# Half of the second weight sums of a seven-product matrix product taken from accumulating DMA to VectorE, with the sums of x and the down passes moved

## The chip, the cores and the metric

The kernel runs on one core of a Trainium2 chip. The time is the device time of one execution in microseconds, and the median of several runs is compared. TensorE (PE in the profile) multiplies; VectorE (DVE), ScalarE (ACT) and GpSimd (POOL) work beside it, and SyncE (SP) issues most of the DMAs. Each engine executes its own instructions in order.

## The reference, cut to what matters

One layer of a trunk on 256 tokens of width 2048, in float32. Two SwiGLU feed-forward stages of width 5632 stand at its ends, with a mixer (a recurrent and an attention branch) between them. The change touches only the feed-forward stages:

```python
def _swiglu(x, w1, w3, w2):
    return (jax.nn.silu(x @ w1) * (x @ w3)) @ w2

x = _layer_norm(ALPHA * x + 0.5 * _swiglu(x, ffn1_w1[i], ffn1_w3[i], ffn1_w2[i]), ln1_g[i], ln1_b[i])
mix = _hybrid_mixer(x, w_in[i], b_gates_m[i], conv_m[i], norm_m[i], w_up_m[i], w_up_sb[i], w_out[i])
x = _layer_norm(ALPHA * x + mix, ln2_g[i], ln2_b[i])
x = _layer_norm(ALPHA * x + 0.5 * _swiglu(x, ffn2_w1[i], ffn2_w3[i], ffn2_w2[i]), ln3_g[i], ln3_b[i])
x = x + jax.nn.sigmoid(x @ w_ple_gate[i]) * (p[i] @ w_ple_proj[i])
```

## The kernel before

Every float32 factor is split into a high and a low part (`hi`, `lo`) of a type that TensorE multiplies faster, and a product of two factors is three matmuls: hi by hi, hi by lo and lo by hi (L1057 to L1059). A weight comes from HBM by DMA as a tile `raw` of 128 x 1024 values, ACT copies it to the high part (L1006) and VectorE subtracts to get the low one (L1010). A **unit** is one weight tile against one half of the tokens: six matmuls, 128 x 512 each.

The width 5632 is cut into eleven chunks of 512. Chunks 0 and 5 are computed plainly: gate (`w1`), then hidden (`w3`). The other nine go through `seven` (L312), which takes the two token halves and the two matrices `w1` and `w3` together as a 2 by 2 block product and forms it with seven products in place of eight. For each of the four **quads** `i` of 512 rows:

- product 1 takes the tile `t`, a quarter of `w1`, as loaded;
- product 5 takes T1: after the split for product 1, `w1.then` adds a quarter of `w3` to `t` in place by an accumulating DMA from GpSimd's queue (`grow`, L328);
- product 6 takes T2: after the split for product 5, `w5.then` adds a second quarter of `w3` to `t`, in the same way;
- product 2 takes a second quarter of `w1` (`b21`), product 4 the sum of `t` and `b21`, made by VectorE (`plus`, L333);
- products 7 and 3 take two quarters of `w3`, one after a sum by VectorE (L333 too).

Products 5, 6, 7 and 3 multiply sums of x in place of x. `form_turn` (L277) forms these sums once per stage and chunk of x, 18 + 5c units of planned time after chunk c of x is transposed (`DELAY["form"]`, L275), by four small VectorE operations, and splits them (L258, L259).

After the last unit of product 5, ACT copies bank E to `e` (L454) and VectorE writes X minus E into the bank B (L448), which product 6 then accumulates onto. Three empty places (`None`, L358) stand between products 5 and 6.

The list `main` (L504) holds the rest of the stage: the plain chunks and the down passes. A down pass `down(c)` multiplies the hidden values of chunk c (transposed by `turn`, L425, to tiles of `hT`) by `w2`, for four column groups `g`, and adds the outcome to `xres` on VectorE (L494): eight additions a pass. `down(5, 7)` sums two chunks in one pass. Before, there are nine passes: 0; 1; 2; 3; 4; 6; 5 and 7; 8 and 9; 10. `weave` (L155) puts the list of the seven-product chunks (`chained`, L352) between the units of `main` in even spacing, empty places counted.

The order of all instructions is written out by the program itself: it walks the list, keeps a planned time (`sched.now`, 1.30 for each unit), and issues turns, transposes and sums when they are due; where a unit needs a tile that isn't made yet, `sched.until` issues what is queued first. Splits are issued up to seven weights ahead (`SPLIT_FFN`). `loads` (L972) issues the weight DMAs ahead as long as pages are left: the pages of activation tiles, the raw tiles and two for each split must stay below `PAGES`, 44. A raw tile counts until the split that frees it (`frees`). A weight whose tile must first be summed has `make`, called while the weight before it or the one before that is split (`make(j + 1)`, `make(j + 2)`); `after` holds it back until another weight is split.

Of the kernel before, what the change touches and what calls it, by code (L numbers as in the profile page):

```python
# [24 lines left out]

PAGES = 44
TEMP_BUFS = 6


RAW_FFN, RAW_MIX, RAW_EDGE = 12, 5, 4  # L30
# [9 lines left out]


DELAY = {
    "after": 14.0, "form": 18.0, "ln_turn": 5.0, "ln_step": 1.7, "h": 8.0, "silu": 6.0, "late": 9.0, "rest": 1.2, "mt": 3.2,
    "sbt": 4.6, "g0": 3.0, "g1": 4.0, "g2": 12.0, "cv0": 1.0, "cv1": 3.5, "cv2": 1.3,
    "m0": 3.0, "m1": 0.6, "m2": 0.6, "m3": 4.6, "m4": 4.6, "s0": 6.6, "s1": 6.7, "s2": 5.0,
}
# [123 lines left out]
def flat(pairs):  # L170
    return [u for p in pairs for u in p]
# [7 lines left out]
def kernel(  # L179
# [7 lines left out]
    x, out = x[0], out[0]  # L187
# [5 lines left out]
    page_pool = ctx.enter_context(tc.tile_pool(name="page", bufs=PAGES))  # L193
    temp_pool = ctx.enter_context(tc.tile_pool(name="temp", bufs=TEMP_BUFS))
    small = ctx.enter_context(tc.tile_pool(name="small", bufs=4))
# [6 lines left out]
    sched = Sched()  # L202
    temps = [0]

    def temp():
        sched.until(lambda: temps[0] < TEMP_BUFS)
        temps[0] += 1
        return temp_pool.tile([P, COL], F32, name="temp", tag="temp")
# [10 lines left out]
    pages = [0]  # L219
# [41 lines left out]
    def transposed(src, act, c, t):  # L261
        ps = misc([P, 4, P])
        for k in range(4):
            nc.tensor.transpose(ps[:, k], src[:, k * P:(k + 1) * P], ident[:])  # L264
        dst = act.get(c, t)
        nc.scalar.copy(dst[:, 0], ps[:])  # L266
        if act.forms:
            if c not in act.whole:
                act.whole[c] = big()
                pages[0] += 1  # L270
            nc.scalar.copy(act.whole[c][:, t * COL:(t + 1) * COL], ps.rearrange("q k s -> q (k s)"))
        nc.vector.tensor_tensor(out=dst[:, 1], in0=ps[:], in1=dst[:, 0], op=ALU.subtract)  # L272
        act.mark(c, t, 4)
        if act.forms and all(act.ready(c, h) for h in range(TT)):
            sched.spawn(form_turn(act, c), DELAY["form"] + 5.0 * c)  # L275

    def form_turn(act, c):  # L277

        a = [act.whole[c][:, t * COL:(t + 1) * COL] for t in range(TT)]
        s12, s34 = temp(), temp()  # L280
        l, r = slice(0, 2 * P), slice(2 * P, 4 * P)
        nc.vector.tensor_tensor(out=s12[:, l], in0=a[1][:, l], in1=a[1][:, r], op=ALU.subtract)
        nc.vector.tensor_tensor(out=s12[:, r], in0=s12[:, l], in1=a[0][:, l], op=ALU.subtract)
        nc.vector.tensor_tensor(out=s34[:, l], in0=a[0][:, l], in1=a[1][:, l], op=ALU.subtract)
        nc.vector.scalar_tensor_tensor(out=s34[:, r], in0=a[0][:, r], scalar=-1.0, in1=s12[:, r],
                                       op0=ALU.mult, op1=ALU.subtract)
        yield 4.0
        pages[0] -= 1
        for h, src in enumerate((s12, s34)):
            dst = act.forms.get(c, h)  # L290
            split_psum(dst[:, 0], dst[:, 1], src.rearrange("q (k s) -> q k s", s=P))
            drop()
            act.forms.mark(c, h, 4)
# [18 lines left out]
    def seven(wa, wb, rows, col0, cols, act, done):  # L312

        n = rows // (4 * P)
        banks = {k: {} for k in "XEBW"}

        def unit(m, i, tile, src, half, sub, bank, first):
            u = Unit(tile, half, banks[bank], src, i, sub, first and i == 0, i == n - 1,
                     lambda ps, t, m=m: done(m, banks))
            u.onto = not first  # L320
            return u

        def quarter(w, i, sub):
            return rows_of(w, (4 * i + sub) * P, col0, cols)

        def grow(raw, src):
            def load():
                nc.gpsimd.dma_start(out=raw.tile[:, :, :cols], in_=src.src, accum_op=ALU.add)  # L328
            return load

        def plus(a, b):
            def make():
                nc.vector.tensor_tensor(out=a.tile[:, :, :cols], in0=a.tile[:, :, :cols], in1=b.tile[:, :, :cols],  # L333
                                        op=ALU.add)
            return make

        one, five, six, two, four, rest = [], [], [], [], [], []
        for i in range(n):
            t, b21 = quarter(wa, i, 0), quarter(wa, i, 2)
            w1, w5, w6 = Weight(t, [t], []), Weight(t, [], []), Weight(t, [], [])  # L340
            w1.then, w5.then = grow(t, quarter(wb, i, 0)), grow(t, quarter(wb, i, 2))
            one.append(unit(1, i, w1, act, 0, 0, "X", True))
            five.append(unit(5, i, w5, act.forms, 0, 0, "E", True))
            six.append(unit(6, i, w6, act.forms, 0, 2, "B", False))
            two.append(unit(2, i, Weight(b21, [b21], []), act, 0, 2, "X", False))
            four.append(unit(4, i, Weight(t, [], [t, b21], plus(t, b21)), act, 1, 2, "E", False))
            b12, b22 = quarter(wb, i, 0), quarter(wb, i, 2)
            rest.append(unit(7, i, Weight(b12, [b12, b22], [b12], plus(b12, b22)), act.forms, 1, 0, "W", False))
            rest.append(unit(3, i, Weight(b22, [], [b22]), act.forms, 1, 2, "B", False))
        return one, five, six, two, four, rest  # L350

    def chained(parts):  # L352

        out = list(parts[0][0])
        for j, (_, five, six, two, four, rest) in enumerate(parts):
            ahead = list(parts[j + 1][0]) if j + 1 < len(parts) else []
            n = len(five)
            out += five + [None] * 3 + six + two[:1]  # L358
            for i in range(n):
                out += two[i + 1:i + 2] + four[i:i + 1] + (ahead[i - 2:i - 1] if i >= 2 else [])  # L360
            ahead = ahead[n - 2:]
            for i, u in enumerate(rest):
                out += [u] + ahead[i:i + 1]
        return out
# [56 lines left out]
    def ffn(w1, w3, w2, act, norm, skew=True, ahead=()):  # L421
# [67 lines left out]
        def down(*chunks):  # L489
            pairs = []  # L490
            for g in range(D // COL):
                def add(ps, t, g=g):
                    xs = xres[t][:, g * COL:(g + 1) * COL]
                    nc.vector.scalar_tensor_tensor(out=xs, in0=ps, scalar=0.5, in1=xs,  # L494
                                                   op0=ALU.mult, op1=ALU.add)
                    if n - 1 in chunks:
                        norm.chunk(t, g)
                pairs += group(w2, [c * COL + r for c in chunks for r in (0, 2 * P)], g * COL, COL, hT, add)
            return pairs

        gate, hidden = zip(*(up(c) for c in (0, 5)))
        program.extend((skewed(gate[0][:SKEW]) if skew else flat(gate[0][:SKEW])) + flat(gate[0][SKEW:]))
        rest, tail = down(8, 9), down(10)
        main = flat(hidden[0] + gate[1] + down(0) + down(1) + down(2) + down(3) + down(4) + hidden[1] + down(6) + down(5, 7))  # L504
        program.extend(main[:8] + weave(main[8:] + flat(rest[:8]), chained([up7(c) for c in (1, 2, 3, 4, 6, 7, 8, 9, 10)])))
        program.append(norm.load)
        program.extend(ahead)
# [307 lines left out]
    for n in (4, 4, 4, 4, 4, 2):  # L815
        program.extend(flat(group(w_in, range(0, D, 2 * P), sq0 + first * DS, n * DS, x1T,
                                  lambda ps, t, f=first, n=n: sb_columns(ps, t, f, n))))
# [138 lines left out]
    pos = {"load": 0, "split": 0, "at": 0, "raw": 0}  # L956

    def mixing():
        j = pos["split"]
        return any(-EDGE <= j - e < EDGE for e, _ in edges) or [m for e, m in edges if e <= j][-1:] == [True]  # L960

    def limits(j):

        if any(-EDGE <= j - e < EDGE for e, _ in edges):
            return RAW_EDGE, SPLIT_EDGE
        mixer = [m for e, m in edges if e <= j][-1:] == [True]
        return (RAW_MIX, SPLIT_MIX) if mixer else (RAW_FFN, SPLIT_FFN)
# [3 lines left out]

    def loads(most=len(raws)):  # L972
        while (pos["load"] < most and pos["raw"] < (4 if pos["at"] < 6 else limits(pos["split"])[0])
               and (mixing() or pages[0] + pos["raw"] + 2 * limits(pos["split"])[1] < PAGES)):
            j = pos["load"]
            r = raws[j]
            r.tile = page_pool.tile([P, 2, COL], F32, name="raw", tag="page")
            for ks in pieces(j):
                nc.sync.dma_start(out=r.tile[:, ks, :r.cols], in_=r.src[:, ks])
                if j == 0 and ks.start == 0:  # L980
                    load_x(0, 1)
            if r.plus is not None:
                nc.gpsimd.dma_start(out=r.tile[:, :, :r.cols], in_=r.plus, accum_op=ALU.add)
            pos["load"] += 1
            pos["raw"] += 1
# [111 lines left out]
```

## Time and profile before

| | |
|---|---|
| median of 3 runs | 2329.43 us (2327.81 to 2337.3) |
| profiled execution, its own time | 2336.99 us |
| span of its instructions | 2335.2 us |
| mean granted TensorE clock | 0.979 |
| first feed-forward stage, seven-product part | about 45 to 720 us |
| second one | about 1510 to 2175 us |

PE busy counts a matmul from its issue to its end, and matmuls overlap, so the share of busy time is not that of the peak. A row of a wait says which instruction waited, for which, for how long in all, how many times and how long at most. The granted clock is 1.00 at full speed.

### The profile page before, as it was taken

How to read it: one execution, taken by the hardware profiler on the slowest of the kernel's cores; microseconds unless marked ns; L12 is line 12 of the kernel's file. 1: busy time of each engine (PE TensorE's matmuls, PEld its weight loads, DVE VectorE, ACT ScalarE, POOL GpSimd, SP SyncE). 2: the span in 40 equal slices, each digit the busy share in tenths (PEclk: the TensorE clock that was granted, in tenths of full speed). 3: DMA queues.
4: the chain of work that ended last, by engine and by line, in shares of the span. 5: the costliest groups of instructions: out<-in, count | busy, mean ns of one | idle time of the engine just before them, and what ended most of it. 6: DMA issues, size and time to landing. Idle time of an engine off the chain costs nothing.

```text
span 2335.2 us, 27582 instructions
## 1 busy us (share of the span) xinstructions
PE 2229.2 (95%) x10017; PEld 1833.4 (79%) x10017; DVE 1730.4 (74%) x1884; ACT 1259.3 (54%) x1471; POOL 223.3 (10%) x191
## 2 busy tenths in 40 slices
PE   9899999999899999999999999999899999988999
PEld 7677877887777788888888888777787787777878
DVE  6888898897787765654445456888788889778883
ACT  6655565664564455544643453556556566555552
POOL 3111111111000000100100000311110111100000
PEclk9999999999999999999999999999999999999999
DMA  9778988989795565565566577578897798978643
GB/s 325 213 219 244 283 241 224 263 222 278 220 284 183 172 190 160 174 185 157 163 189 191 178 237 234 158 208 234 238 284 224 228 263 232 269 219 263 240 148 104
DMA packets 267208, 510.21 MB, mean 218 GB/s; under 512 B 16000, under 2 KB 25024, under 8 KB 267072
## 3 DMA queue, kind: packets, MB, share of 16 engines
q1 hardware_dynamic: 227904, 432.95, 56.3%
q0 software_dynamic: 39168, 75.51, 18.0%
q8 instruction: 78, 1.28, 0.2%
q14 instruction: 58, 0.48, 0.1%
HBM read 506.30 MB, written 2.10 MB: 218 GB/s over the span
## 4 chain that ended last, share of the span: by engine, by line
PE 52%; issue 15%; DMA 6%; DVE 3%; POOL 2%; ACT 0%; POOLq 0%; ACTq 0%; DVEq 0%
PE mm L1057 15%; PE mm L1059 15%; PE mm L1058 15%; DMA raw<-in_ffn_w_dram 5%; POOL raw L328 2%; PE seeded L1057 2%; PE seeded L1058 2%; PE seeded L1059 1%; PE ms L264 1%; DVE split L1010 1%; DVE xres L403 1%; DMA temp<-in_conv_m_dram 0%; DVE xres L401 0%; DVE xres L404 0%; ACT split L1006 0%
## 5 line engine op out<-in xcount | busy, mean ns | idle before, releaser
L1010 DVE TENSOR_TENSOR split<-raw,split 128x1024 fp32r<-128x1024 f32 (+1 forms) x1037 | 1212.6, 1204 | 350.7 <-ACT split L1006 329.0
L1006 ACT CAST split<-raw 128x1024 fp32r<-128x1024 f32 (+1 forms) x1037 | 1038.1, 1037 | 619.1 <-DMA raw<-in_ffn_w_dram 164.9
L1057 PE MATMUL mm<-split,actT 128*128 128x512 f32 (+2 forms) x2704 | 1059.0, 392 | 18.5 <-ACT actT L258 12.8
L1059 PE MATMUL mm<-split,actT 128*128 128x512 f32 (+2 forms) x2704 | 1049.0, 388 | 12.3 <-DVE actT L272 11.5
L1058 PE MATMUL mm<-split,actT 128*128 128x512 f32 (+2 forms) x2704 | 1047.5, 387 | 5.5 <-DVE split L1010 5.4
L1057 PEld LDWEIGHTS mm<-split,actT 128*128 128x128 f32 x2704 | 513.1, 190 | 121.2 <-ACT actT L258 14.5
L1059 PEld LDWEIGHTS mm<-split,actT 128*128 128x128 f32 x2704 | 512.4, 190 | 121.8 <-DVE actT L272 16.9
L1058 PEld LDWEIGHTS mm<-split,actT 128*128 128x128 f32 x2704 | 513.2, 190 | 106.8 <-DVE split L1010 8.3
L328 POOL DMA_DIRECT2D raw<-in_ffn_w_dram x144 | 175.2, 1228 | 1079.3 <-DVE split L1010 822.3
L1057 PE MATMUL seeded<-split,actT 128*128 128x512 f32 x432 | 177.7, 411 | 52.8 <-DVE seeded L448 52.8
L333 DVE TENSOR_TENSOR raw<-raw 128x1024 f32<-128x1024 f32 x144 | 175.4, 1218 | 54.8 <-DMA raw<-in_ffn_w_dram 54.8
L1058 PE MATMUL seeded<-split,actT 128*128 128x512 f32 x432 | 175.3, 406 | 4.7 <-DVE split L1010 4.7
L1059 PE MATMUL seeded<-split,actT 128*128 128x512 f32 x432 | 173.9, 403 | 0.0
L1057 PEld LDWEIGHTS seeded<-split,actT 128*128 128x128 f32 x432 | 85.0, 197 | 75.2 <-DVE seeded L448 57.8
L266 ACT CAST actT<-ms 128x512 fp32r<-128x512 f32 x84 | 49.1, 588 | 105.7 <-PE ms L264 89.3
L1058 PEld LDWEIGHTS seeded<-split,actT 128*128 128x128 f32 x432 | 85.1, 197 | 24.2 <-DVE split L1010 7.3
L494 DVE SCALAR_TENSOR_TENSOR xres<-mm,xres 128x512 f32<-128x512 f32 x144 | 97.9, 683 | 6.5 <-PE mm L1059 6.5
L1059 PEld LDWEIGHTS seeded<-split,actT 128*128 128x128 f32 x432 | 84.8, 196 | 18.3
L272 DVE TENSOR_TENSOR actT<-ms,actT 128x512 fp32r<-128x512 f32 x84 | 57.1, 684 | 25.2 <-ACT actT L266 13.7
L418 POOL TENSOR_SCALAR xres<-xres 128x512 f32<-128x512 f32 x16 | 28.7, 1836 | 320.0 <-DVE xres L401 300.5
L236 ACT ACTIVATE temp<-mm 128x512 f32<-128x512 f32 (+1 forms) x36 | 20.7, 576 | 48.9 <-PE mm L1059 48.9
L236 ACT ACTIVATE big<-mm 128x512 f32<-128x512 f32 x20 | 12.0, 598 | 55.8 <-PE mm L1059 55.8
(124 smaller groups left out, 641.3 us busy)
## 6 DMA issues: line engine op xcount, KB each, us to landing
raw<-in_ffn_w_dram SPq DMA_DIRECT2D x527, 512.0 KB, 7.9
raw<-in_w_in_dram SPq DMA_DIRECT2D x168, 512.0 KB, 3.8
raw<-in_ffn_w_dram POOLq DMA_DIRECT2D x144, 512.0 KB, 9.7
raw<-in_w_out_dram SPq DMA_DIRECT2D x32, 512.0 KB, 5.2
raw<-in_w_ple_gate_dram SPq DMA_DIRECT2D x24, 512.0 KB, 4.7
raw<-in_w_up_m_dram SPq DMA_DIRECT2D x16, 512.0 KB, 3.7
raw<-in_w_up_sb_dram SPq DMA_DIRECT2D x16, 512.0 KB, 4.3
raw<-in_w_ple_gate_dram SPq DMA_DIRECT2D x16, 256.0 KB, 4.5
```

The lines of the kernel that those rows point to most:

```text
L236: nc.scalar.activation(out, in_, func, **kw)
L266: nc.scalar.copy(dst[:, 0], ps[:])
L272: nc.vector.tensor_tensor(out=dst[:, 1], in0=ps[:], in1=dst[:, 0], op=ALU.subtract)
L328: nc.gpsimd.dma_start(out=raw.tile[:, :, :cols], in_=src.src, accum_op=ALU.add)
L333: nc.vector.tensor_tensor(out=a.tile[:, :, :cols], in0=a.tile[:, :, :cols], in1=b.tile[:, :, :cols], op=ALU.add)
L418: nc.gpsimd.tensor_scalar(out=xs, in0=xs, scalar1=ALPHA, scalar2=None, op0=ALU.mult)
L494: nc.vector.scalar_tensor_tensor(out=xs, in0=ps, scalar=0.5, in1=xs, op0=ALU.mult, op1=ALU.add)
L1006: nc.scalar.copy(hi[:, ks], r[:, ks])
L1010: nc.vector.tensor_tensor(out=lo[:, ks], in0=r[:, ks], in1=hi[:, ks], op=ALU.subtract)
L1057: nc.tensor.matmul(ps, hi, w[0][:, k, :u.cols], start=first, stop=False, skip_group_check=u.onto)
L1058: nc.tensor.matmul(ps, hi, w[1][:, k, :u.cols], start=False, stop=False, skip_group_check=u.onto)
L1059: nc.tensor.matmul(ps, lo, w[0][:, k, :u.cols], start=False, stop=last, skip_group_check=u.onto)
```

## The change

- T2 of the quads 1 and 3 of each chunk is no longer formed by an accumulating DMA. The quarter of `w3` is loaded to a tile of its own by a plain DMA from SP's queue, and VectorE adds it to `t` (`plus`, L333) after the split for product 5. Quads 0 and 2 stay as they were.
- The sums of x are due 14 + 3c after the transposes in place of 18 + 5c.
- Eight empty places (`FORMED`) stand between product 1 and product 5 of the first seven-product chunk.
- The down passes become eight: 0 and 1; 2; 3; 4; 6 and 5; 7; 8 and 9; 10. (The nine before are named above.)
- Weight loads stop one page sooner (`SPARE`).

```diff
+FORMED = 8
+SPARE = 1
...
-    "after": 14.0, "form": 18.0, "ln_turn": 5.0, "ln_step": 1.7, "h": 8.0, "silu": 6.0, "late": 9.0, "rest": 1.2, "mt": 3.2,
+    "after": 14.0, "form": 14.0, "ln_turn": 5.0, "ln_step": 1.7, "h": 8.0, "silu": 6.0, "late": 9.0, "rest": 1.2, "mt": 3.2,
...
-            sched.spawn(form_turn(act, c), DELAY["form"] + 5.0 * c)
+            sched.spawn(form_turn(act, c), DELAY["form"] + 3.0 * c)
...
             w1, w5, w6 = Weight(t, [t], []), Weight(t, [], []), Weight(t, [], [])
-            w1.then, w5.then = grow(t, quarter(wb, i, 0)), grow(t, quarter(wb, i, 2))
+            w1.then = grow(t, quarter(wb, i, 0))
+            if i % 2:
+                b = quarter(wb, i, 2)
+                w6 = Weight(t, [b], [b], plus(t, b), w5)
+            else:
+                w5.then = grow(t, quarter(wb, i, 2))
...
-        out = list(parts[0][0])
+        out = list(parts[0][0]) + [None] * FORMED
...
-        main = flat(hidden[0] + gate[1] + down(0) + down(1) + down(2) + down(3) + down(4) + hidden[1] + down(6) + down(5, 7))
+        main = flat(hidden[0] + gate[1] + down(0, 1) + down(2) + down(3) + down(4) + hidden[1] + down(6, 5) + down(7))
...
-               and (mixing() or pages[0] + pos["raw"] + 2 * limits(pos["split"])[1] < PAGES)):
+               and (mixing() or pages[0] + pos["raw"] + 2 * limits(pos["split"])[1] < PAGES - SPARE)):
```

## The prediction

> **What bounds the kernel now.** I read the busy times first, then who TensorE waits for, then the places of those waits in order of time.
>
> ```profile
> span 2335.2 us, 27582 instructions
> ...
> PE 2229.2 (95%) x10017; PEld 1833.4 (79%) x10017; DVE 1730.4 (74%) x1884; ACT 1259.3 (54%) x1471; POOL 223.3 (10%) x191
> ```
>
> TensorE (PE) is the bound. A gain can only come from its gaps or from the time in which its clock is low. The waits of PE over the whole span:
>
> ```profile
> PE seeded L1057 <- DVE seeded L448: 52.8, 12, 6.6
> PE mm L1057 <- ACT actT L258: 12.8, 3, 7.9
> PE mm L1059 <- DVE actT L272: 11.5, 10, 2.7
> PE mm L1057 <- ACT actT L266: 5.7, 4, 2.5
> PE mm L1058 <- DVE split L1010: 5.4, 5, 2.0
> PE seeded L1058 <- DVE split L1010: 4.7, 5, 1.7
> ```
>
> The columns are microseconds in all, times, longest. The largest is the wait for L448, which seeds the bank of product 6 (X minus E) after product 5. It strikes 12 of the 18 seven-product chunks. What is late there is seen in chunk 4, in the timelines of PE, DVE, ACT and POOL:
>
> ```profile
> 296.89 0.80 PE L1057 MATMUL seeded<-split,actT 128*128 128x512 f32 x1 [5.52 <-DVE seeded L448]
> ...
> 296.14 0.69 DVE L448 TENSOR_TENSOR seeded<-mm,temp 128x512 f32<-128x512 f32 x1
> ...
> 284.94 1.05 ACT L1006 CAST split<-raw 128x1024 fp32r<-128x1024 f32 x1 [5.29 <-DMA raw<-in_ffn_w_dram]
> ...
> 288.96 1.05 ACT L1006 CAST split<-raw 128x1024 fp32r<-128x1024 f32 x1 [2.44 <-DMA raw<-in_ffn_w_dram]
> 292.79 1.99 ACT L1006 CAST split<-raw 128x1024 fp32r<-128x1024 f32 x2 [2.78 <-DMA raw<-in_ffn_w_dram]
> 294.69 0.58 ACT L454 COPY temp<-mm 128x512 f32<-128x512 f32 x1
> ...
> 276.80 1.20 POOL L328 DMA_DIRECT2D raw<-in_ffn_w_dram  x1 [17.20 <-DVE split L1010]
> 279.07 2.44 POOL L328 DMA_DIRECT2D raw<-in_ffn_w_dram  x2 [1.07 <-DVE split L1010]
> ```
>
> The four accumulating DMAs that form T2 are issued within some 6 us. They land one after another, 4.0 and 3.8 us apart (284.94, 288.96, 292.79). ACT works in order: the copy of E (L454, 0.58 us) stands behind the split of the third T2 and starts at 294.69. PE had run dry at 296.89 - 5.52 = 291.37. So the third landing of four sets the end of this wait.
>
> A stall costs twice, since the granted clock (next to last but two columns) is halved after it. Here are the first and the last of the nine slow stretches behind L448 waits, and the sum of the nine:
>
> ```profile
> 147.91:150.63 2.72, 2.72 (x6) 2.14 (x7) 2.72 (x4) 1.12 (x2) 0.00 (x0) 0.50 0.03 6
> ...
> 2128.89:2134.20 5.31, 5.31 (x13) 4.15 (x14) 4.35 (x5) 2.99 (x3) 0.00 (x0) 0.50 0.07 27
> sum 37.80, PE 37.79 PEld 29.63 DVE 34.80 ACT 19.96 POOL 0.00; mean PE 4.20 PEld 3.29 DVE 3.87 ACT 2.22 POOL 0.00
> ```
>
> 37.8 us at 0.50 lose half: 18.9 us. The first of them also gives the pitch: 2.72 us for 6 matmuls is 0.453 each at half clock, 0.227 at full clock, and 1.36 us for a unit of six.
>
> **T2 of the odd quads.** 36 accumulating DMAs go, two of four in each chunk; 36 plain loads on SP's queue and 36 sums at L333 come. The sums' price and what the fewer down passes return (16 fewer L494):
>
> ```profile
> L333 DVE TENSOR_TENSOR raw<-raw 128x1024 f32<-128x1024 f32 x144 | 175.4, 1218 | 54.8 <-DMA raw<-in_ffn_w_dram 54.8
> ...
> L494 DVE SCALAR_TENSOR_TENSOR xres<-mm,xres 128x512 f32<-128x512 f32 x144 | 97.9, 683 | 6.5 <-PE mm L1059 6.5
> ```
>
> 36 x 1.218 - 16 x 0.683 = 32.9 us more VectorE work. The third T2 (quad 2) becomes the second of two accumulations, so it lands about one interval sooner, 3.8 us. Twelve waits of 52.8 / 12 = 4.4 us mean would leave 0.6 us each; but the short ones can't give 3.8:
>
> ```profile
> 510.16 0.50 PE L1057 MATMUL seeded<-split,actT 128*128 128x512 f32 x1 [1.55 <-DVE seeded L448]
> ...
> 147.91 0.79 PE L1057 MATMUL seeded<-split,actT 128*128 128x512 f32 x1 [2.68 <-DVE seeded L448]
> ```
>
> So the long ones keep more. I leave 13 us in all: **-40**, between -15 (worked out under the first rival) and -53. Of the slow clock I take 15 of 18.9: **-15** (ends 4 and 19). The 2.68 us wait was followed by the slow stretch at 147.91; the 1.55 us wait was not (its first matmul took 0.50, not 0.79).
>
> The Trainium skill (TensorE: Matmul & The Clock Gate, Part 1) has the clock halve after an idle window of about 3.4 us. The 2.68 us row was slow already, so the trace bears the rule out only roughly. By it, leftover waits of about 1 us cost no clock at all, and this term would be -19.
>
> The new sums lie on VectorE before product 6, where it idles for ACT (60.6 us in this stretch, and 26.9 for DMA):
>
> ```profile
> 45.00:720.00 675.00, 630.85 (x2729) 514.26 (x2727) 566.68 (x559) 396.87 (x427) 86.51 (x71) 0.96 0.87 248
> ...
> L1010 DVE TENSOR_TENSOR split<-raw,split 128x1024 fp32r<-128x1024 f32 x349 | 415.3, 1219 | 74.2 <-ACT split L1006 60.6 <-PE mm L1059 7.6 <-PE mm L1058 2.7
> L333 DVE TENSOR_TENSOR raw<-raw 128x1024 f32<-128x1024 f32 x72 | 87.7, 1218 | 26.9 <-DMA raw<-in_ffn_w_dram 26.9
> ```
>
> VectorE is busy 566.7 of 675 us; 16 more in a stage some 22 us shorter is 583 of 653, 89%. I charge **+3** (0 to +33, if it were the bound all along). A sum stands in VectorE's FIFO ahead of splits and of L448, all of which wait if its b is late.
>
> **SP's queue and pages.** Each added load takes a page until its split, and SPARE takes one page off what may be loaded ahead. PE's waits for L1010 (5.4 + 4.7 = 10.1 us, in ten) show what late weights cost now. I charge half of it again, **+5** (0 to +20: twice what is there). For it speak 36 shorter transfers:
>
> ```profile
> q1 hardware_dynamic: 66675, 129.38, 55.9%
> q0 software_dynamic: 19505, 37.59, 30.9%
> ```
>
> Of 675 us of the 16 DMA engines that is 1.53 us for each plain 0.524 MB and 2.91 for each accumulating one.
>
> **Sums of x sooner, product 5 later.** Chunk 1's product 5 waits for the sums of x:
>
> ```profile
> 66.79 0.80 PE L1057 MATMUL mm<-split,actT 128*128 128x512 f32 x1 [7.87 <-ACT actT L258]
> ...
> 66.12 1.13 ACT L258 CAST actT<-temp 128x512 fp32r<-128x512 f32 x2
> ...
> 66.79:72.56 5.77, 5.65 (x12) 3.69 (x13) 5.67 (x10) 3.13 (x5) 0.00 (x0) 0.50 0.44 81
> ...
> 1529.28:1533.30 4.02, 3.41 (x8) 2.44 (x9) 3.76 (x5) 2.46 (x3) 0.00 (x0) 0.63 1.00 214
> ```
>
> The delay falls from 18 + 5c to 14 + 3c: 4, 6, 8 and 10 us sooner. Counted along the program list, eight empty places move the first unit of product 5 from place 31 to 36: five units of 1.36 us, 6.8 us. For sum 2, which is 7.87 us late, that makes 14.8. At stake: 12.8 plus slow clock of 2.9 and 4.02 x 0.37 = 1.5, in all 17.2. ACT's splits of T2 stand ahead of L258 too, so not all goes: **-15** (-8 to -17).
>
> **Down passes.** Joined passes need their second chunk sooner. Counting units between a chunk's last product and its first down unit: chunk 4 goes from 9 to 4, chunk 3 from 19 to 11, chunk 9 from 13 to 12, and chunk 1 from 41 to 3 (less the unit itself: two matmul units, 2.7 us). Chunk 4 shows what too few units cost:
>
> ```profile
> 366.02 0.55 PE L1057 MATMUL mm<-split,actT 128*128 128x512 f32 x1 [1.82 <-ACT actT L266]
> 368.11 0.80 PE L1059 MATMUL mm<-split,actT 128*128 128x512 f32 x1 [1.11 <-DVE actT L272]
> 369.98 1.05 PE L264 MATMUL ms<-ident,temp 128*128 128x128 f32 x4
> 371.71 0.80 PE L1057 MATMUL mm<-split,actT 128*128 128x512 f32 x1 [0.67 <-ACT actT L266]
> 371.08 0.58 ACT L266 CAST actT<-ms 128x512 fp32r<-128x512 f32 x1 [1.16 <-PE ms L264]
> ...
> 371.71:376.20 4.49, 4.49 (x11) 3.31 (x12) 2.81 (x4) 1.04 (x1) 0.00 (x0) 0.50 0.28 73
> ```
>
> 3.6 us of waits and 2.2 of slow clock, 5.8. Its L266 stood behind a T2 split, which now comes sooner; against that it has 5 units less: **0** (-8 to +8). Chunk 1 gets the same wait new. First half: transposes 0.6, L266 0.58 and L272 0.68 leave 1.8 exposed. Second half: L481 (0.68) comes first, with one split (1.2) ahead of it, 3.1. With 1.5 of slow clock that is 6.4 in each of the two feed-forward stages: **+13** (0, if the order hides it, to +22). Chunks 3 and 9 are forced slightly early in their second half, about 1 us each: **+4** (0 to +8). down(6, 5) leaves 12 units, 16 us, for chunk 5's transposes, due at 8 and 10: 0.
>
> **Sum:** -40 - 15 + 3 + 5 - 15 + 0 + 13 + 4 = **-45 us**. The profiled execution took 2336.99 us (1.8 outside its span), so 2292; it lies 7.6 above the median of the runs shown, 2329.43, from which the same difference gives **2284**.
>
> **Rivals.** *The DMA engines are shared anyway.* The b loads run in the very window of the accumulations, where the engines are full:
>
> ```profile
> 208.00:222.00 14.00, 9.37 (x44) 7.43 (x42) 8.52 (x10) 5.69 (x8) 1.20 (x1) 0.91 0.97 230
> 222.00:252.00 30.00, 29.42 (x124) 24.21 (x125) 29.25 (x31) 18.42 (x19) 2.41 (x2) 0.93 0.58 169
> ```
>
> Then T2 lands sooner only by 2.91 - 1.53 = 1.4 us: 12 x 1.4 gives -17 for -40 and -4 for the clock, in all -11: **2318**. Against it: pages limit the loads, so a b takes the place of another load there. This is what the Trainium skill says of queues (DMA: Bandwidth & Descriptors, Issuing engines are not separate DMA queues): all issuers share 16 engines. The 0.97 at 208 us agrees; whether a b displaces another load no row shows. Chance 0.14.
>
> *VectorE becomes the bound.* It has 29.25 of 30 us in the stretch from 222. If the added 33 us came fully on the path: -45 + 30 = -15, **2314**. Against it: 8.52 of 14 us just before, where the sums stand. Chance 0.11.
>
> *The b loads are as late as the DMA they replace, without more*: L448 gains nothing, -15 + 25 = +10, **2339**. Chance 0.10.
>
> *Slower: the new sum waits at the head of VectorE's queue for its b.* L333's waits cost 54.8 us in 20, 2.74 each; one page less makes b late. 26 of 36 late give 71 - 45 = +26, **2355**; it decides against the change from 17 late ones on (17 x 2.74 = 47). For it: those 20 waits exist, seldom on PE's path. Chance 0.09.
>
> **How the numbers follow.** The forecast has 0.56, with a range of 2260 to 2308. The 80% range is **2250 to 2322**: at the low end L448, clock and sums of x give all they have (-53 - 19 - 17 + 17 + 3 - 8 = -77, 2252); the first two rivals lie inside, the last two are left out. Half a per cent, about what a measurement here tells from no change, is 11.6 us. The first rival lies on that bound and is halved: faster 0.56 + 0.07 + 0.07 = 0.70; within 0.07 + 0.04 + 0.08 = 0.19; slower 0.02 + 0.09 = 0.11.
>
> **What would show it.** Right: PE's wait for L448 below 20 us, no wait of several us for L258, new waits of 1 to 3 us for L266 and L272 near 125 to 145 us, 108 issues on POOL's queue, L333 x180, L494 x128. Wrong: L448 above 35 us (accumulations land as before), L333's wait for DMA above 100 us, PE's waits for L1010 above 30 us, or VectorE without gaps while PE waits.

## The result and the profile after

The changed kernel takes 2307.29 us (median of 4 runs, 2302.39 to 2309.71) against 2330.69 us before. The ratio is 0.9893, with a 95% interval of 0.9866 to 0.992: faster by 1.07%, some 25 us. The forecast was 45 us. The time lies in the narrower range of the forecast (2260 to 2308) by 0.7 us only, and the sign is right, but a little more than half of the expected gain was had. The profiled execution (2302.39 us) has a span 34.8 us shorter than that of before. Some 11 us of that are scatter between executions: this one lies 4.9 us below the median of its kernel, and the profiled one of before (2336.99 us) 6.3 above its own.

The page after, its span and the busy times:

```profile
span 2300.4 us, 27598 instructions
...
PE 2217.5 (96%) x10017; PEld 1825.2 (79%) x10017; DVE 1755.3 (76%) x1904; ACT 1257.2 (55%) x1471; POOL 179.1 (8%) x155
```

Seven lines were added to the code, so L448 is now L455 (the seeding subtraction), L266 and L272 are L268 and L274 (the copies of transposed tiles), L1010 is L1017 and L333 is L335 (the sums). Who TensorE waited for (microseconds in all, times, longest):

```profile
PE mm L1066 <- DVE actT L274: 22.3, 13, 3.0
PE mm L1064 <- ACT actT L268: 21.8, 12, 3.9
PE seeded L1064 <- DVE seeded L455: 17.7, 9, 2.8
PE mm L1065 <- DVE split L1017: 5.8, 4, 2.4
PE seeded L1065 <- DVE split L1017: 3.5, 2, 1.8
```

Three things are to be read here. The wait for the seeding went from 52.8 to 17.7 us. The wait for the sums of x (12.8 us before) is no longer in the list. The waits for the transposed tiles went from 11.5 + 5.7 = 17.2 to 22.3 + 21.8 = 44.1 us: 27 us of the gain went there. The mean granted clock rose from 0.979 to 0.987.

The additions did what the diff says. The page's groups and its DMA issues:

```profile
L335 DVE TENSOR_TENSOR raw<-raw 128x1024 f32<-128x1024 f32 x180 | 219.1, 1217 | 77.0 <-DMA raw<-in_ffn_w_dram 76.8
...
L501 DVE SCALAR_TENSOR_TENSOR xres<-mm,xres 128x512 f32<-128x512 f32 x128 | 86.6, 683 | 7.2 <-PE mm L1066 7.2
...
raw<-in_ffn_w_dram POOLq DMA_DIRECT2D x108, 512.0 KB, 9.1
```

VectorE waits 76.8 us for DMA at its sums, where it waited 54.8 before, and there are 36 sums more.

What a wait for a transposed tile is made of can be seen at chunk 3, in the timelines of PE, ACT and VectorE after the change:

```profile
289.49 0.60 PE L266 MATMUL ms<-ident,temp 128*128 128x128 f32 x4
294.00 0.50 PE L1064 MATMUL mm<-split,actT 128*128 128x512 f32 x1 [3.91 <-ACT actT L268]
...
289.96 1.04 ACT L1013 CAST split<-raw 128x1024 fp32r<-128x1024 f32 x1 [1.33 <-DVE raw L335]
293.36 0.59 ACT L268 CAST actT<-ms 128x512 fp32r<-128x512 f32 x1 [2.36 <-DVE split L1017]
...
288.66 1.21 DVE L335 TENSOR_TENSOR raw<-raw 128x1024 f32<-128x1024 f32 x1
289.79 3.49 DVE L1017 TENSOR_TENSOR split<-raw,split 128x1024 fp32r<-128x1024 f32 x3
```

The transposes (L266) are done at 290.1. ACT's copy L268 starts only at 293.36, just when the third of VectorE's splits ends (289.79 + 3.49 = 293.28). The copy reads nothing of a split. What it needs and a split gives free is a page for the new tile; that it was the page is argued from this, not shown. PE lost 3.91 us there. The waits of chunk 4 (L268 and L274, near 355 and 1800 us) grew too, from 8.0 us in both stages to 11.4.

### The profile page after: what moved, and what is told of

Same layout as the page of the kernel before. It is cut to its first block, busy times and chain, and to the rows that moved or that the text cites. A ratio compares the mean times of both kernels' runs of the same rounds, so it can differ in the third digit from the quotient of the medians.

```text
span 2300.4 us, 27598 instructions
## 1 busy us (share of the span) xinstructions
PE 2217.5 (96%) x10017; PEld 1825.2 (79%) x10017; DVE 1755.3 (76%) x1904; ACT 1257.2 (55%) x1471; POOL 179.1 (8%) x155
## 5 line engine op out<-in xcount | busy, mean ns | idle before, releaser
L1017 DVE TENSOR_TENSOR split<-raw,split 128x1024 fp32r<-128x1024 f32 (+1 forms) x1037 | 1206.6, 1203 | 263.0 <-ACT split L1013 253.9
L1064 PE MATMUL mm<-split,actT 128*128 128x512 f32 (+2 forms) x2704 | 1056.8, 391 | 22.3 <-ACT actT L268 21.8
L1066 PE MATMUL mm<-split,actT 128*128 128x512 f32 (+2 forms) x2704 | 1049.3, 388 | 22.3 <-DVE actT L274 22.3
L335 DVE TENSOR_TENSOR raw<-raw 128x1024 f32<-128x1024 f32 x180 | 219.1, 1217 | 77.0 <-DMA raw<-in_ffn_w_dram 76.8
L330 POOL DMA_DIRECT2D raw<-in_ffn_w_dram x108 | 131.4, 1227 | 1085.7 <-DVE split L1017 731.6
L1064 PE MATMUL seeded<-split,actT 128*128 128x512 f32 x432 | 172.6, 400 | 17.7 <-DVE seeded L455 17.7
L1065 PE MATMUL seeded<-split,actT 128*128 128x512 f32 x432 | 171.3, 397 | 3.5 <-DVE split L1017 3.5
L1066 PE MATMUL seeded<-split,actT 128*128 128x512 f32 x432 | 170.8, 395 | 0.0
L1064 PEld LDWEIGHTS seeded<-split,actT 128*128 128x128 f32 x432 | 83.0, 192 | 38.6 <-DVE seeded L455 21.5
L268 ACT CAST actT<-ms 128x512 fp32r<-128x512 f32 x84 | 49.1, 589 | 108.4 <-PE ms L266 95.9
L1065 PEld LDWEIGHTS seeded<-split,actT 128*128 128x128 f32 x432 | 82.7, 191 | 21.4 <-DVE split L1017 4.3
L1066 PEld LDWEIGHTS seeded<-split,actT 128*128 128x128 f32 x432 | 82.8, 192 | 17.7
L501 DVE SCALAR_TENSOR_TENSOR xres<-mm,xres 128x512 f32<-128x512 f32 x128 | 86.6, 683 | 7.2 <-PE mm L1066 7.2
L274 DVE TENSOR_TENSOR actT<-ms,actT 128x512 fp32r<-128x512 f32 x84 | 57.1, 684 | 30.7 <-ACT actT L268 20.4
```

Source lines behind the costliest of these rows:

```text
L1017: nc.vector.tensor_tensor(out=lo[:, ks], in0=r[:, ks], in1=hi[:, ks], op=ALU.subtract)
L1064: nc.tensor.matmul(ps, hi, w[0][:, k, :u.cols], start=first, stop=False, skip_group_check=u.onto)
L1065: nc.tensor.matmul(ps, hi, w[1][:, k, :u.cols], start=False, stop=False, skip_group_check=u.onto)
L1066: nc.tensor.matmul(ps, lo, w[0][:, k, :u.cols], start=False, stop=last, skip_group_check=u.onto)
```

## The experiments

All ratios are to runs of the kernel before that were taken together with the run, on the same chip. Four runs at a time share their runs of before, so a comparison between groups goes by ratios. A "theory" is one of the two accounts that the expectation before each run sets against each other.

**The T2 edit alone.** The kernel before, with this part only:

```diff
-            w1.then, w5.then = grow(t, quarter(wb, i, 0)), grow(t, quarter(wb, i, 2))
+            w1.then = grow(t, quarter(wb, i, 0))
+            if i % 2:
+                b = quarter(wb, i, 2)
+                w6 = Weight(t, [b], [b], plus(t, b), w5)
+            else:
+                w5.then = grow(t, quarter(wb, i, 2))
```

> The kernel before with the T2 edit alone (quads 1 and 3 by a plain load and a VectorE sum); sums of x, empty places, down passes and pages as before. Order theory (the forecast fell short because chunks 1, 3, 4 and 9 are asked for by their down pass before their transposes are due, which the empty places and the joined passes cause): the waits for the seeding subtraction fall from 52.8 to under 20 us and their slow clock goes, no new waits for the transposed hidden tiles: 2280 to 2292 us, faster than the changed kernel although it lacks the 18 us of the sums of x. VectorE theory (the added sums hold up VectorE, and the copies of the hidden tiles wait behind them in ScalarE's queue wherever they stand): waits for hidden tiles of 30 us or more here too, 2300 to 2312 us.

Measured: 2280.34 us, ratio 0.9762 (0.9746 to 0.9778). One part of the change is more than twice as good as the whole of it. The time is that of the order theory, though the seeding waits stayed just above its 20 us. PE's waits in this run:

```profile
PE seeded L1062 <- DVE seeded L453: 23.2, 8, 3.8
PE mm L1064 <- DVE actT L272: 15.1, 12, 2.7
PE mm L1062 <- ACT actT L258: 10.6, 4, 6.4
```

The seeding falls from 52.8 to 23.2 us. The waits for transposed tiles don't rise (17.2 before, 16.5 here), though the added sums are all there: so the sums alone don't make them. Chunk 4 loses its slow clock: before, the granted clock was 0.50 for 10.24 us there in each stage (from 366.35 and 1830.67 us); here it is 1.00 throughout (340 to 380 and 1775 to 1815 us). How the third T2 of chunk 3 now arrives, in the timelines of POOL and ACT of this run:

```profile
201.55 1.20 POOL L328 DMA_DIRECT2D raw<-in_ffn_w_dram  x1 [18.23 <-DVE split L1015]
204.95 1.20 POOL L328 DMA_DIRECT2D raw<-in_ffn_w_dram  x1 [2.20 <-DVE split L1015]
...
214.80 1.99 ACT L1011 CAST split<-raw 128x1024 fp32r<-128x1024 f32 x2 [3.21 <-DMA raw<-in_ffn_w_dram]
216.70 0.58 ACT L459 COPY temp<-mm 128x512 f32<-128x512 f32 x1
```

It is issued at 204.95, and its split starts at 214.80, 9.9 us later. ACT's split still waits for it, but for two landings in place of three.

**The rest without T2, with the nine passes:** all four T2 by accumulating DMA, so that the sums of x sooner, the empty places and the spare page are left. The edit is shown against the changed kernel.

```diff
-            if i % 2:
-                b = quarter(wb, i, 2)
-                w6 = Weight(t, [b], [b], plus(t, b), w5)
-            else:
-                w5.then = grow(t, quarter(wb, i, 2))
+            w5.then = grow(t, quarter(wb, i, 2))
...
-        main = flat(hidden[0] + gate[1] + down(0, 1) + down(2) + down(3) + down(4) + hidden[1] + down(6, 5) + down(7))
+        main = flat(hidden[0] + gate[1] + down(0) + down(1) + down(2) + down(3) + down(4) + hidden[1] + down(6) + down(5, 7))
```

> The changed kernel with T2 as before (all four by accumulating DMA) and the nine down passes as before: what is left is the sums of x sooner, the eight empty places and SPARE. Order theory: the wait for the sums of x goes (-17 us), the seeding waits stay near 50 us, chunks 3 and 4 are forced as in the changed kernel (+8 to +14): 2318 to 2328 us. VectorE theory: no added sums, so chunks 3 and 4 wait no more than before: 2308 to 2316 us.

Measured: 2352.35 us, ratio 1.0079 (1.006 to 1.0097): slower, outside both expectations. PE's waits:

```profile
PE seeded L1059 <- DVE seeded L450: 60.0, 15, 7.1
PE mm L1059 <- ACT actT L268: 17.3, 8, 4.6
PE mm L1061 <- DVE actT L274: 14.8, 12, 2.7
```

The wait for the sums of x is gone, but the seeding waits rose from 52.8 to 60.0 and those for the copies of transposed tiles from 5.7 to 17.3. Chunks 3 and 9 wait for their copies here too (3.2 and 9.1 us over both stages), where they had no such wait before. The VectorE theory had these down to the added sums; there are none here. With all of it, these three parts cost 0.8% where the forecast had a gain of 15 us for the sums of x. The joined passes without the T2 edit weren't tried.

**The changed kernel with the nine passes:**

```diff
-        main = flat(hidden[0] + gate[1] + down(0, 1) + down(2) + down(3) + down(4) + hidden[1] + down(6, 5) + down(7))
+        main = flat(hidden[0] + gate[1] + down(0) + down(1) + down(2) + down(3) + down(4) + hidden[1] + down(6) + down(5, 7))
```

> The changed kernel with the nine down passes as before. Order theory: the waits of chunk 1 for its transposed hidden tiles (5.2 and 5.0 us and 2 us of slow clock) go, those of chunks 3, 4 and 9 stay; sixteen additions at 0.683 us come back off the path: 2291 to 2300 us. VectorE theory: 11 us more VectorE work, so 2307 us or slower.

Measured: 2297.38 us, ratio 0.9836 (0.9822 to 0.9851), 0.57% or 13 us below the changed kernel's 0.9893; the intervals don't overlap. This is the order theory's outcome. So fewer passes save 11 us of VectorE work and, by the ratios, cost 13 us in all. The waits for L268 fall from 21.8 to 13.4 us; chunk 1's go wholly. The two profiled executions differ by less, 3.8 us of span: the seeding waits go the other way, from 17.7 us with eight passes to 24.4 with nine.

**The hidden half of chunk 5 sooner,** with chunks 0 and 1 in passes of their own, in the changed kernel:

```diff
-        main = flat(hidden[0] + gate[1] + down(0, 1) + down(2) + down(3) + down(4) + hidden[1] + down(6, 5) + down(7))
+        main = flat(hidden[0] + gate[1] + down(0) + down(1) + down(2) + hidden[1] + down(3) + down(4) + down(6, 5) + down(7))
```

> The changed kernel with chunks 0 and 1 in passes of their own again and the hidden half of chunk 5 moved ahead of the pass of chunk 3, so that chunks 1, 3 and 4 have 31, 52 and 42 units between their last product and their down pass (3, 11 and 4 in the changed kernel). Two more pages are held between the passes of chunks 3 and 6. Order theory: the waits for the hidden tiles of these three chunks go, about 25 us with their slow clock and chunk 4's old ones too: 2277 to 2290 us. VectorE theory: the time moves to other waits on VectorE, the split and the seeding: 2300 us or more.

Measured: 2287.53 us, ratio 0.9794 (0.9778 to 0.981). PE's waits:

```profile
PE seeded L1064 <- DVE seeded L455: 23.8, 12, 3.8
...
PE seeded L1065 <- DVE split L1017: 11.7, 8, 2.7
PE mm L1065 <- DVE split L1017: 10.6, 6, 2.8
...
PE mm L1064 <- ACT actT L268: 1.9, 2, 1.0
```

With room before their down passes, the waits of chunks 1, 3 and 4 for L268 go (21.8 to 1.9 us): the order makes them. Chunk 9, whose order is unchanged, still waits some 3.9 us in each stage. But the waits for splits rise from 9.3 to 22.3 us and those for the seeding from 17.7 to 23.8. This order holds two more pages of hidden tiles for longer, and pages are what the loads live on. That called for a test of the pages by themselves.

**On top of the T2 edit, one part each.** First the sums of x sooner (`"form": 14.0` and `+ 3.0 * c`):

> T2 edit plus the earlier sums of x (14 + 3c), no empty places, no spare page, nine passes. T2 alone gave 2280 us and left 12.5 us of waits for the sums of x with about 4 us of slow clock. If the delay alone cures them: 2265 to 2272 us. If the sums were late because of the queue in front of them and not because of their due time, or if they only push splits back: 2278 to 2285 us.

Measured: 2272.71 us, ratio 0.9739 (0.972 to 0.9758), against 0.9762 (0.9746 to 0.9778) for T2 alone. The intervals overlap, so a gain of 0.2% is possible but not settled; the time falls between the two expectations. PE's wait for L258 falls from 10.6 to 4.3 us.

Then the spare page (`< PAGES - SPARE`, with `SPARE = 1`):

> T2 edit plus the spare page alone. The three parts beside T2 cost 17 us together, with T2 and without it. Page theory (one page less ahead makes weights late; the waits for the split and for the sums at VectorE grow): 2288 to 2297 us. Order theory (the empty places cost it, since they bring chunks 3, 4 and 9 too close to their down passes): 2278 to 2284 us.

Measured: 2292.01 us, ratio 0.9827 (0.9805 to 0.985): 0.65% slower than T2 alone, as the page theory had it. VectorE's wait at its sums is the witness, in T2 alone and here (the line numbers differ by one):

```profile
DVE raw L333 <- DMA raw<-in_ffn_w_dram: 48.5, 22, 4.4
```

```profile
DVE raw L334 <- DMA raw<-in_ffn_w_dram: 76.7, 27, 9.5
```

One page less in the loads' count makes VectorE wait 28 us longer for weights; PE's waits for splits go from 5.3 to 13.1 us.

Then the eight empty places (`[None] * FORMED`, with `FORMED = 8`):

> T2 edit plus the eight empty places alone. Order theory: the waits for the sums of x (12.5 us and their slow clock) mostly go, and chunks 3, 4 and 9 are forced early, with waits of 1 to 4 us for the copies of their hidden tiles in each stage as in the changed kernel (about 25 us with slow clock): 2285 to 2295 us. Page theory: no page is taken, so only the gain is seen: 2264 to 2272 us.

Measured: 2290.18 us, ratio 0.9813 (0.9794 to 0.9832): 0.5% slower than T2 alone. PE's waits:

```profile
PE mm L1065 <- DVE actT L273: 17.9, 11, 3.0
PE mm L1063 <- ACT actT L267: 15.5, 8, 3.9
PE seeded L1063 <- DVE seeded L454: 13.3, 8, 3.4
```

This is the order theory's outcome. L267 (the copy of transposed tiles) is at 15.5 us, where T2 alone has 1.4. Chunk 3 waits 3.9 us for it in each stage and chunk 9 some 3.9 us, as in the changed kernel; with T2 alone neither waits. What this run wins at the seeding (23.2 to 13.3 us) and at the sums of x it loses again at these copies. The mean granted clock is 0.985 against 0.990, half a per cent less, which is as much as the whole loss.

Last the hidden half of chunk 5 sooner, on T2 alone (with chunks 6 and 5 in one pass, and 7 by itself):

> T2 edit plus the hidden half of chunk 5 ahead of the pass of chunk 3, passes 0; 1; 2; 3; 4; 6 and 5; 7; 8 and 9; 10; no empty places, delay and pages as before. Order theory: chunk 4's waits (7 us in T2 alone, 2 us of slow clock) go, nothing is added: 2268 to 2274 us. Page theory (two more pages held between the passes of chunks 3 and 6 make weights late there, as the waits for the split in the run with the early hidden half suggest): 2280 to 2290 us.

Measured: 2291.58 us, ratio 0.9819 (0.9798 to 0.9839): near the page theory's outcome (2280 to 2290). Chunk 4's waits go, VectorE's wait for DMA rises from 48.5 to 76.0 us, and PE's waits for splits rise from 5.3 to 15.8.

**On top of T2 and the sooner sums, four more.** All T2 by VectorE (`if True:` for `if i % 2:`):

> T2 edit plus the earlier sums of x (2272.7 us), but all four T2 of a chunk by a plain load and a VectorE sum. VectorE theory (the sums are near the bound): 44 us more VectorE work, the waits for the seeding and the splits grow: 2285 us or more. If the accumulating DMAs are what the remaining 22 us of seeding waits come from: 2250 to 2265 us. Two more pages in use for each chunk would show as a longer wait of VectorE's sums for DMA (44 us now).

Measured: 2307.6 us, ratio 0.9877 (0.9857 to 0.9897): 1.4% slower than with half of them. PE's largest wait and ACT's:

```profile
PE seeded L1062 <- DVE seeded L453: 38.0, 11, 4.3
```

```profile
ACT split L1011 <- DVE raw L333: 170.6, 96, 6.5
```

This is the VectorE theory's outcome. No accumulation stands between products 5 and 6 any more, and yet the seeding waits are 38 us: the splits of ACT wait 170.6 us for VectorE's sums (83.2 with half of them). Here VectorE has taken the DMA's place. Its wait for DMA is almost unchanged (47.0 against 44.2), so late loads don't seem to be the reason.

One page more in the loads' count (`< PAGES + 1`; the pool itself keeps 44):

> T2 edit plus the earlier sums of x, with weight loads allowed one page more (one less cost 11.7 us). Page theory: VectorE's wait for DMA at its sums falls below 44 us, 2263 to 2270 us. If 44 is the true number of pages, the load only waits at the queue for its page in place of the program's count, and nothing changes: 2270 to 2276 us.

Measured: 2265.47 us, ratio 0.9698 (0.9676 to 0.972), the fastest kernel of the study, faster than both kernels compared. Against the run without the added page (0.9739, 0.972 to 0.9758) the intervals just touch. PE's largest wait, and VectorE's for DMA:

```profile
PE seeded L1062 <- DVE seeded L453: 18.1, 11, 3.7
```

```profile
DVE raw L333 <- DMA raw<-in_ffn_w_dram: 39.0, 15, 4.6
```

The other quads by VectorE (`if i % 2 == 0:`):

> T2 edit plus the earlier sums of x, with quads 0 and 2 by VectorE and quads 1 and 3 by accumulating DMA. The copy of product 5's bank stands behind the split of the third T2, quad 2, in ScalarE's queue. Landing theory: quad 2 waits for no accumulation now, so the seeding waits fall from 22 us to under 10, and what is left shows later, at the split of quad 3: 2255 to 2268 us. If the copy waits for VectorE instead (its sum and splits in order), the seeding waits stay at 20 us or grow: 2272 to 2285 us.

Measured: 2276.52 us, ratio 0.9749 (0.9726 to 0.9772), not to be told from the odd quads' 0.9739. The seeding waits stay:

```profile
PE seeded L1062 <- DVE seeded L453: 20.2, 12, 3.5
```

Quad 2 waits for no accumulating landing here, and yet the seeding waits as long. Why is seen at chunk 3, in the timelines of POOL, ACT and VectorE:

```profile
200.38 1.20 POOL L328 DMA_DIRECT2D raw<-in_ffn_w_dram  x1 [19.78 <-DVE split L1015]
...
209.88 2.95 ACT L1011 CAST split<-raw 128x1024 fp32r<-128x1024 f32 x3 [2.94 <-DMA raw<-in_ffn_w_dram]
212.74 0.57 ACT L459 COPY temp<-mm 128x512 f32<-128x512 f32 x1
...
210.97 3.50 DVE L1015 TENSOR_TENSOR split<-raw,split 128x1024 fp32r<-128x1024 f32 x3 [0.56 <-ACT split L1011]
214.38 0.69 DVE L453 TENSOR_TENSOR seeded<-mm,temp 128x512 f32<-128x512 f32 x1
```

ACT's wait ends at 209.88 with the landing of the accumulation issued at 200.38, quad 1's, the first of the two. Two more splits and the copy of product 5's bank follow in ACT's queue, and the subtraction L453 then stands behind VectorE's three splits. In 11 of the 12 seeding waits of this run, one of the three instructions ahead of the copy waited for an accumulating landing. So it isn't the landing of quad 2 by itself: here a landing of another quad, ahead of the copy in ACT's queue, holds it up as long.

The changed kernel with no spare page (`SPARE = 0`):

> The changed kernel with no spare page, everything else of the change kept. Page theory: the 11.7 us that the page cost beside T2 alone come back, 2293 to 2298 us, and VectorE's wait for DMA at its sums falls from 77 to about 50 us. If the page only mattered without the empty places and the joined passes: 2303 to 2309 us.

Measured: 2306.95 us, ratio 0.9871 (0.9846 to 0.9895): no difference to the changed kernel that can be measured (0.9893, 0.9866 to 0.992). VectorE's wait for DMA does fall, from 76.8 to 50.6 us. PE's waits don't:

```profile
PE mm L1064 <- ACT actT L268: 24.2, 12, 3.9
PE seeded L1064 <- DVE seeded L455: 19.1, 9, 4.6
PE mm L1066 <- DVE actT L274: 15.7, 11, 3.0
PE seeded L1065 <- DVE split L1017: 8.9, 6, 2.2
```

A likely reading, which no run shows: where PE stands at chunks 1, 3, 4 and 9 anyway, late weights have time to come. In any case the costs of the parts don't add up.

## Why the prediction was right in sign and twice too large

The runs split the 25 us in three, along one path from before to the changed kernel (1% is 23.3 us; each measured part is uncertain by some 4 to 7 us):

| part | forecast | measured, from the ratios |
|---|---|---|
| T2 of the odd quads (L448, clock, VectorE) | -40 - 15 + 3 = -52 | 0.9762 - 1: -55 |
| sums of x, empty places, spare page (with chunks 3, 4 and 9) | -15 + 4 + 0 + 5 = -6 | 0.9836 - 0.9762: +17 |
| eight passes (chunk 1) | +13 | 0.9893 - 0.9836: +13 |

What the prediction named as signs of being right was all seen: a seeding wait below 20 us (17.7), none for the sums of x, 1.5 us waits near 135 us, 108 issues from GpSimd. Those signs covered the gains and chunk 1; none of them watched the chunks behind the empty places. The forecast's +5 for late weights stands whole in the second row, though the added loads of T2 are in it too.

- **T2: the mechanism was right; that the size fits is in part luck.** With T2 alone the seeding wait fell by 29.6 us (-40 forecast), in the changed kernel by 35.1. The nine slow stretches behind these waits cost 21.3 us before, counted as half of PE's busy time in them (18.9 in the prediction, which left out parts of some). With T2 alone six are left, which cost 11.5: a gain of 9.8 (-15 forecast). Both terms came out smaller with T2 alone; the rest came from places where nothing was forecast or a cost was. Chunk 4 lost 9.2 us of waits and slow clock, and PE's waits for splits fell from 10.1 to 5.3. That half of the landings was the cause of the fall is borne out by the run with T2 alone; most of what is left still hangs on the landings that remain (the run with the even quads).
- **Chunk 1: its waits were right.** They are 5.2 and 5.0 us in the two stages (forecast 4.9 each), with 2.8 us of slow clock in the second stage only (forecast 1.5 in each). The 13 us by the ratio of the runs agree; as other waits moved the opposite way, that this whole-kernel figure fits so well may be chance.
- **Sums of x and empty places: this step failed.** The waits for the sums did go, all 12.8 us. But the forecast booked the whole gain to the two edits together and priced the delay that the empty places bring to chunks 3 and 9 at 4 us ("forced slightly early in their second half, about 1 us each"). Chunk 3 waited 3.91 and 3.92 us, chunk 9 4.0 us in each stage, and every one of them drew slow clock behind it: 15.8 us of waits and 8.0 of slow clock, 24 us where 4 were forecast. The run with T2 and the empty places alone has the same there, 15.7 and 8.6. Chunk 4, at 0 in the forecast, did end where it was before (16.4 us of waits and slow clock before, 16.1 after), but that gives back the 9 us that T2 alone had won there. With T2 alone in place, the empty places cost 12 us (0.9762 to 0.9813); the sums sooner are worth about -5 (to 0.9739), which is not settled. The forecast took the copy of a transposed tile to start as soon as its transposes end; at chunk 3 it started 3.3 us after them, when VectorE's splits were done.
- **The page: mis-sized, and it depends on the rest.** +5 us were charged. On T2 alone it costs 15 us (0.9762 to 0.9827), in the changed kernel nothing that can be measured; PE's waits for splits there are 9.3 us, where 15 were forecast.
- **VectorE +3 us: no run measures this term by itself.** With T2 alone PE's waits for VectorE's splits fell. As a rival it came true only when all four sums were given to it: 38 us of seeding waits and 1.4%.
- **The rival of the shared DMA engines fell.** It had the seeding wait fall by 17 us; it fell by 29.6 and more.

**The clock** is the last point. Two seeding waits of the changed kernel in PE's timeline, and stretches of 3.41 us around them (PE's busy time is the first figure after the comma, the granted clock the last but two):

```profile
574.06 0.50 PE L1064 MATMUL seeded<-split,actT 128*128 128x512 f32 x1 [2.49 <-DVE seeded L455]
...
2020.55 0.50 PE L1064 MATMUL seeded<-split,actT 128*128 128x512 f32 x1 [2.80 <-DVE seeded L455]
```

```profile
571.68:575.10 3.42, 1.04 (x5) 0.86 (x6) 2.93 (x4) 3.42 (x6) 0.00 (x0) 1.00 1.06 397
575.10:578.51 3.41, 3.41 (x10) 2.63 (x9) 3.41 (x6) 1.79 (x2) 0.00 (x0) 0.50 0.31 112
...
2015.53:2018.94 3.41, 2.21 (x10) 1.50 (x8) 3.41 (x4) 2.60 (x5) 0.00 (x0) 1.00 1.06 361
2018.94:2022.35 3.41, 1.80 (x8) 1.48 (x9) 3.41 (x5) 3.41 (x5) 0.00 (x0) 1.00 1.05 393
2022.35:2025.77 3.42, 3.42 (x17) 2.82 (x16) 3.42 (x5) 0.77 (x1) 0.00 (x0) 1.00 0.29 104
```

The shorter wait was followed by half clock, the longer one wasn't. The traces show why. In all 14 of them, each of the 374 changes of the granted clock lies on a grid of 3.413 us that runs on unbroken through the span. The clock goes by how long PE idled within one cell of that grid (roughly, since the ends of matmuls are modelled). Of the cells at full clock in which PE idled more than 57.5% (1.96 us), all 160 were followed by half clock; of those in which it idled less than 47.5% (1.62 us), none of 8892; in between, 20 of 66. The wait of 2.49 us lies almost whole in one cell, where PE was busy for 1.04 us of 3.41. That of 2.80 us falls across two, with 2.21 and 1.80 us busy. The Trainium skill (TensorE: Matmul & The Clock Gate, Part 1) has a window of some 3.4 us that runs freely. The grid agrees with it; but where the skill speaks of an idle window, a window that was idle for little more than half was enough here. So a left-over wait of 1 us by itself costs no clock, as the prediction had it; whether one of 2 to 3 us does depends on where it falls.

## What to carry to other kernels

A wait of the bound engine that follows an in-order queue stuck behind one of several landings is worth removing, and half of the transfers given to another engine can be enough; all of them may make that engine the next queue. Edits that move the program list are not free because they add no work: count, for every consumer behind the shift, how many units are left between its producer and its first use, and price the copy behind the splits that it may have to wait for, not behind its input alone. Try the parts of such a change singly: here one part gave more than twice the gain of the whole, and the best kernel (ratio 0.9698) counts one page more for loads where the change took one away.

## What the runs showed of the hardware that was not expected

The granted clock changed only on a grid of 3.413 us, and every cell in which TensorE idled more than 57.5% was followed by half clock. A single page of 0.5 MB among 44 is worth 0.65% where weights are what is late: VectorE's wait for DMA went from 48.5 to 76.7 us with one page less, and from 44.2 to 39.0 with one more. An accumulating transfer of 0.524 MB still took 9.1 us from issue to landing in the median (9.7 before) although there were a quarter fewer of them.
